# Weight tiles on multiples of 512 bytes, values fetched by head, stores spread: one change to a two-layer attention trunk

## The chip, the cores and the metric

One core of a Trainium2 chip runs the whole program in one launch. The metric is the device time of that launch in microseconds (us). The kernel before has a median of 1944.94 us over 3 runs (1943.95 to 1949.24).

Engines: PE is TensorE (matrix products; PEld its weight loads), DVE is VectorE, ACT is ScalarE, POOL is GpSimd, SP issues most transfers. A matrix product has a stationary operand (128x128, loaded into the array) and a moving one (128 partitions x up to 512 columns).

## The reference

Two layers on 512 tokens of width 2048, all in float32. Layer 0 is differential attention with ALiBi (8 heads, two score maps each, values of 256), layer 1 forgetting attention (16 heads of 128) on keys, values and forget gates projected once from the output of layer 0. Each layer shifts and scales its input by vectors computed from `c`, gates its output with SiLU, and ends in a residual layer norm.

```python
c_act = silu(c)
for l in range(2):
    shift, scale, gate = split(c_act @ w_mod[l] + b_mod[l], 3)
    h = x * (1 + scale) + shift
    if l == 0:
        q, k, v, g = split(h @ a_w_in, 4)
        a = softmax(q1 @ k1.T + alibi) - lam * softmax(q2 @ k2.T + alibi)
        y = (rms_norm(a @ v) * (1 - lam_init) * silu(g)) @ a_w_out
    else:
        hk = x * (1 + scale_kv) + shift_kv
        k, v, zf = split(hk @ kv_w)                  # once
        F = cumsum(log_sigmoid(zf + b_f))
        q, g = split(h @ b_w_in, 2)
        p = softmax(q @ k.T + F[t] - F[s], causal)
        y = (p @ v * silu(g)) @ b_w_out
    x = layer_norm(sqrt(2) * x + gate * y)
```

(`DN_ALPHA` is 4 to the power of 1/4, the square root of 2.)

## The kernel before, in words

**Products.** Every large product is made of three in the fast 32-bit format: a float32 operand is split into a rounded part `hi` and the rest `lo`, and hi·hi, hi·lo and lo·hi are summed in PSUM (`products`, L340, lines L342 to L344; in the opening stage `product`, L889, line L894). Tokens lie transposed in 16 pairs `hh`, `hl` of 128 x 512.

**Weights.** `WeightStream` (L173) loads tiles of weights into four buffers `wst` on SP's queue, casts them to `whi` on ACT (L242) and subtracts to `wlo` on DVE (L243); both have three buffers. All these tiles have 1056 columns of 4 bytes, 4224 bytes in a partition, because the narrow pair (below) needs 4 x 264 columns; all others use 1024 of them, as two k-tiles of 512. In the program of before the pool of weights begins on a multiple of 512; `whi` lies 0, 128 and 256 bytes past a multiple of 512 in its three buffers, `wlo` 384, 0 and 128 bytes. The pools of tokens (`hh`, `hl`) and of 2048-byte tiles (`kpool`, tag K, where the last products' `held` weights lie too) are on multiples of 512, and so are all slices of 128 columns of them. The pool of the layer-0 attention starts 256 bytes past a multiple, that of the middle part (`npool`) puts its token sums `su` 128 bytes past one.

**Groups.** `group` (L488) runs one tile of weights after the other (eight steps of two k-tiles) over four PSUM banks. In a column group (Q, K; `natural=False`) a 128-column slice of the weight tile is stationary and the 512 tokens move; in a row group (V, gates, output projections) a slice of 128 tokens is stationary and the 512 weight columns move. A step is 4 banks x 2 k-tiles x 3 = 24 products; after each bank's 6 products, a burst, `tick` (L472) takes the next entry of a list `pieces`: score, softmax, turning and value pieces of the attention of the heads before, which so run between the bursts. `background` streams the modulation vectors on DVE the same way: products with `cact` are summed over partitions by turning 512 columns in blocks of 32 and reducing them (`mod_rows`, L627: `V.transpose` L638, `V.tensor_reduce` L639).

**The middle.** After layer 0 the values' columns are computed partly as two factored pairs of blocks (`seven_products`, L1716: seven products of half blocks in place of eight, from sums of tokens made in `combine`, L1669). First the wide pair (512 columns each), then the narrow one (264 columns: 248 of values and 16 of forget-gate logits). Each ends by storing eight blocks into `v_dram` from ACT's queue (`store`, L1727, issue at L1729). The last 16 columns of the narrow one are copied to `fcols` (L1731); `forget_logits` (L1819) turns them on PE as an entry of `pieces` in the next group.

**Layer 1.** For each of eight pairs of heads a group projects Q and gates. In its last step the values of the pair (128 partitions x 4 blocks x 256 columns) come from `v_dram` into `vld` (`load_pair`, L1941) and are split to `vbh`, `vbl` (`split_pair`, L1950, by `split`, L336, whose lines are L337 on ACT and L338 on DVE); the pieces of the pair run in the next group (`attention_pair`, L2060).

**Order.** The opening stage is written out by hand for four engines (L41 to L44). After it the framework orders each engine's instructions and gives a tile's buffer out again when its last reader is done; each engine then works strictly in that order, so that an instruction that waits holds back those behind it, transfers on the same queue included.

Of the kernel before, what the change touches and what calls it, by code (L numbers as in the profile page):

```python
# [172 lines left out]
class WeightStream:  # L173
# [24 lines left out]
    def tile(self, name, dtype, bufs):  # L198
        return self.pool.tile([P, 1056], dtype, name=name, tag=name, bufs=bufs)
# [77 lines left out]
def tile_yoco(  # L277
# [77 lines left out]
    ones = const.tile([P, P], F32, name="ones")  # L355
    G.memset(ones, 1.0)
# [15 lines left out]
    pcol = const.tile([P, 38], F32, name="pcol")  # L372
# [22 lines left out]
    def load_parameters():  # L395
        prow = rows["p"] = kpool.tile([P, T], F32, name="prow", tag="K")[:38, 0:P]
        nc.sync.dma_start(prow[0:16, :], ln_g[0].rearrange("(a p) -> a p", p=P))
        nc.sync.dma_start(prow[16:32, :], ln_b[0].rearrange("(a p) -> a p", p=P))
        for k, lam in enumerate((a_lam_q1, a_lam_q2, a_lam_k1, a_lam_k2)):
            nc.sync.dma_start(prow[32 + k : 33 + k, :], lam)  # L400
        nc.sync.dma_start(prow[36:38, :], a_subln_g[0].rearrange("(a p) -> a p", p=P))

    def parameter_columns():
        pt = tr_bank()
        PE.transpose(pt[:, 0:38], rows["p"], ident[0:38, 0:38])
        V.tensor_copy(pcol, pt[:, 0:38])
# [220 lines left out]
    def mod_rows(pool, dst, bias, ones_at):  # L627
# [6 lines left out]
        def steps(n, acc):  # L634
            if n == 0:
                red.append(pool.tile([P, P], F32, name="mred", tag="mred", bufs=1)[:, 0 : 16 * last])
            t = pool.tile([P, 512], F32, name="mturn", tag="mturn", bufs=1)
            V.transpose(t, acc)  # L638
# [22 lines left out]
    with tc.tile_pool(name="start", bufs=2, reuse_waits="tile") as sp, tc.manual_schedule(engines=MANUAL):  # L661
# [164 lines left out]
        def op_o(i):  # L826
            if any(r not in d_list[: cnt["d"]] for r in d_list if r[0] == i):
                return False
            if any(r not in e_list[: cnt["e"]] for r in e_list if r[0] == i) or pm_of(i) is None:
                return False  # L830
            nk = sets[i][1]
            for v in range(2):
                for q in range(nk):
                    PE.matmul(
                        pms[i][:, nk * v + q : nk * v + q + 1], acc2[i][:, v, q * P : (q + 1) * P], ones[:, 0:1],
                        start=not rows_pe[i], stop=True, skip_group_check=True,
                    )
            return True
# [159 lines left out]
    for dst, src, col, bias, one in (  # L998
# [4 lines left out]
        steps = mod_rows(ap, dst, bias[col : col + n * D], one)  # L1003
# [7 lines left out]
    def vectors(pool, wanted):  # L1011
        segs = []
        for dst, src, col, bias, one in wanted:
            n = len(one)
            steps = mod_rows(pool, dst, bias[col : col + n * D], one)
# [39 lines left out]
    def attention_a(h, lead=3, late=(), spread=False):  # L1055
# [5 lines left out]
        def score(i, comp):  # L1061
            def fn():
# [450 lines left out]
    def open_n():  # L1513
# [3 lines left out]
        zp.extend((pool, None, pool.tile([P, TB, 4, 6], F32, name="nstats")))  # L1517
# [145 lines left out]
    fcols = npool.tile([P, TB, B_HEADS], F32, name="fcols")  # L1663
# [51 lines left out]

    def seven_products(one, two):  # L1716
# [10 lines left out]
        def store(t, b, col):  # L1727
            n = w if col == c0 else nv
            nc.scalar.dma_start(v_dram[b * P : (b + 1) * P, col : col + n], t[:, :n])  # L1729
            if n < w:  # L1730
                S.copy(fcols[:, b, :], t[:, n:w])  # L1731
                fz["cols", b] = fcols[:, b, :]
# [6 lines left out]
        for a in range(8 // per):  # L1739
            tiles = ws.get(one, a)  # L1740
            for k in range(per):
# [3 lines left out]
                add(p1, lambda b: plain(2 * s, b), tiles, k, s == 0, s == 7)  # L1745
        p2 = banks((partial(tr_bank, "p2"), partial(o_bank, "p2")))
# [16 lines left out]
        for s in range(8):  # L1763
# [21 lines left out]
            if last:  # L1785
# [25 lines left out]
    F = const.tile([P, TB, B_HEADS], F32, name="F")  # L1811
# [7 lines left out]
    def forget_logits():  # L1819
        pt = tr_bank()  # L1820
        for b in range(TB):
            PE.transpose(pt[0:B_HEADS, b * P : (b + 1) * P], fz["cols", b], ident)
# [73 lines left out]
    pieces.extend([None] * 3 + [forget_logits, None, forget_sums] + [None] * 14 + [columns_of_f])  # L1896
# [43 lines left out]

    def load_pair(p):  # L1941
        v = bp.tile([P, TB, 256], F32, name="vld", tag="vld", bufs=1)
        nc.sync.dma_start(v, v_dram[:, 256 * p : 256 * (p + 1)].rearrange("(j p) e -> p j e", p=P))
        cur[p, "vld"] = v
# [5 lines left out]
    def split_pair(p):  # L1950
        vh = bp.tile([P, TB, 256], F32R, name="vbh", tag="vbh", bufs=1)
        vl = bp.tile([P, TB, 256], F32R, name="vbl", tag="vbl", bufs=1)
        split(vh, vl, cur[p, "vld"])
        cur[p, "vB"] = (vh, vl)
        for hd in (2 * p, 2 * p + 1):
# [104 lines left out]
    def attention_pair(p):  # L2060
        sa, ra, da, ta, na, va = attention_b(2 * p)
        sb, rb, db, tb, nb, vb = attention_b(2 * p + 1)
        if p == 7:

            return [
                None, None, sa[0], sa[1], ra[0], [sa[2], ra[1]], da[0], [sa[3], da[1]], [ra[2], ta[0]], [sb[0], ta[1]],
# [4 lines left out]
            [], [], [sa[0]], [sa[1]], [ra[0]], [sa[2], ra[1]], [da[0]], [sa[3], da[1]], [ra[2]], [sb[0], ta[0]],  # L2071
# [207 lines left out]
```

## Time and profile before

| | |
|---|---|
| median of 3 runs | 1944.94 us |
| the profiled execution | 1943.87 us |
| its span | 1942.1 us |
| PE busy | 1925.2 us, 8827 products |
| DVE, ACT, POOL busy | 1432.8, 768.6, 2.3 us |
| HBM traffic | 206 GB/s over the span |

How to read it: a page of the profile has the busy time of each engine, the span in slices, and the chain of work that ended last. Views answer to a part of it. A row of the timeline has the start in us, the duration in us, the engine, the line, the operation, the tiles (out<-in), the shape and a count. A row of groups has line, engine, operation, tiles, shape and count, then the time busy and the mean ns of one, then the idle time ahead of it. A row of waits has who waited for whom, us in total, times, and the longest. A row of stages has the window, its length, and for PE, PEld, DVE, ACT and POOL the busy time with the count; then the granted PE clock, the share of time that the transfer engines are busy, and GB/s. A row of one tile has the operation and count, min/median/max ns, and first and last start. Products overlap: a product's own 0.39 us reaches into the next, so that the distance between starts is what counts.

### The profile page before, as it was taken

To read this page: it belongs to the slowest core of one execution; us is meant where nothing else is said; L and a number is where in the kernel's file an instruction comes from. 1 tells how busy PE (TensorE), PEld (TensorE's weight loads), DVE (VectorE), ACT (ScalarE), POOL (GpSimd) and SP (SyncE) were. 2 spreads that over 40 slices of the span, in tenths; PEclk is the share of its full clock that TensorE was granted. 3 is DMA by queue.
4 is the path that set the end of the run, shared out by engine and by line. 5 is a ranking of instruction groups with operands and counts; after the bars stand their busy time and mean duration, and the time that the engine had idled before them with its cause. 6 is when DMAs were issued, how large, how long until landed. Compare 5 with 4: busy or idle time off the path is not lost.

```text
span 1942.1 us, 25642 instructions
## 1 busy us (share of the span) xinstructions
PE 1925.2 (99%) x8827; PEld 1581.7 (81%) x8827; DVE 1432.8 (74%) x2665; ACT 768.6 (40%) x1304; POOL 2.3 (0%) x11
## 2 busy tenths in 40 slices
PE   8999999999999999999999999999999999999998
PEld 6888888888888888888888888888888888888887
DVE  7893578777776768657687876868866666687978
ACT  3656344333332334521265543224344434453122
POOL 0000000000000000000000000000000000000000
PEclk9999999999999999999999999999999999999999
DMA  9993566676767676476658678776654455555852
GB/s 347 385 322 94 157 189 188 207 236 187 232 192 227 196 222 182 125 259 221 195 175 288 193 213 282 268 260 192 215 162 149 145 153 156 152 153 182 310 166 107
DMA packets 346770, 402.23 MB, mean 207 GB/s; under 512 B 77016, under 2 KB 254324, under 8 KB 345360
## 3 DMA queue, kind: packets, MB, share of 16 engines
q1 hardware_dynamic: 342960, 395.20, 64.0%
q10 hardware_dynamic: 3680, 5.40, 0.9%
q8 instruction: 69, 1.13, 0.2%
q14 instruction: 61, 0.50, 0.1%
HBM read 363.46 MB, written 37.04 MB: 206 GB/s over the span
## 4 chain that ended last, share of the span: by engine, by line
PE 93%; DVE 3%; DMA 2%; SPq 1%; issue 0%; ACT 0%; ACTq 0%; DVEq 0%
PE acc L343 25%; PE acc L344 25%; PE acc L342 25%; PE acc L894 4%; PE sc L894 2%; PE sc L342 2%; PE sc L344 2%; PE sc L343 2%; PE o L342 1%; PE o L344 1%; PE o L343 1%; PE o L894 1%; SPq L742 1%; DVE wlo L243 1%; DMA v_dram<-vfirst 0%
## 5 line engine op out<-in xcount | busy, mean ns | idle before, releaser
L242 ACT CAST whi<-wst 128x1024 fp32r<-128x1024 f32 (+2 forms) x299 | 310.3, 1039 | 598.2 <-PE acc L344 240.7
L243 DVE TENSOR_TENSOR wlo<-wst,whi 128x1024 fp32r<-128x1024 f32 (+2 forms) x299 | 361.4, 1210 | 215.3 <-ACT whi L242 212.9
L344 PE MATMUL acc<-hh,wlo 128*128 128x512 f32 x1184 | 469.1, 396 | 0.0
L343 PE MATMUL acc<-hl,whi 128*128 128x512 f32 x1184 | 468.1, 395 | 0.0
L342 PE MATMUL acc<-hh,whi 128*128 128x512 f32 x1184 | 465.0, 393 | 0.0
L342 PE MATMUL acc<-whi,hh 128*128 128x512 f32 (+1 forms) x912 | 358.1, 393 | 0.2 <-DVE htmp L1762 0.2
L343 PE MATMUL acc<-wlo,hh 128*128 128x512 f32 (+1 forms) x912 | 355.2, 389 | 0.0
L344 PE MATMUL acc<-whi,hl 128*128 128x512 f32 (+1 forms) x912 | 353.7, 388 | 0.0
L342 PEld LDWEIGHTS acc<-hh,whi 128*128 128x128 f32 x1184 | 224.8, 190 | 48.3 <-issue 0.5
L344 PEld LDWEIGHTS acc<-hh,wlo 128*128 128x128 f32 x1184 | 222.3, 188 | 49.6
L343 PEld LDWEIGHTS acc<-hl,whi 128*128 128x128 f32 x1184 | 222.6, 188 | 47.0
L344 PEld LDWEIGHTS acc<-whi,hl 128*128 128x128 f32 x912 | 171.1, 188 | 39.3 <-DVE hl L1585 0.2
L342 PEld LDWEIGHTS acc<-whi,hh 128*128 128x128 f32 x912 | 171.3, 188 | 37.5 <-DVE htmp L1762 0.6
L343 PEld LDWEIGHTS acc<-wlo,hh 128*128 128x128 f32 x912 | 171.5, 188 | 34.4
L612 DVE SCALAR_TENSOR_TENSOR macc<-ms,cact,macc 128x512 f32<-128x512 f32 x180 | 134.0, 745 | 20.1 <-DMA ms<-in_kv_w_mod_dram 11.8
L792 DVE SCALAR_TENSOR_TENSOR sacc<-sms,cact,sacc 128x512 f32<-128x512 f32 (+1 forms) x128 | 90.0, 703 | 5.0 <-DMA sms<-in_w_mod_dram 1.4
L559 DVE SCALAR_TENSOR_TENSOR macc<-ms,cact,macc 128x1024 f32<-128x1024 f32 x60 | 76.8, 1281 | 13.0 <-DMA ms<-in_w_mod_dram 12.5
L1088 ACT ACTIVATE e<-e,mn 128x128 f32<-128x128 f32 (+3 forms) x64 | 36.0, 563 | 113.5 <-DVE mn L1084 106.8
L1987 ACT ACTIVATE eb<-eb,mnb 128x128 f32<-128x128 f32 (+1 forms) x64 | 36.0, 562 | 69.2 <-DVE mnb L1984 68.8
L894 PE MATMUL acc<-wlo,hh 128*128 128x512 f32 x128 | 50.2, 401 | 0.1
L894 PE MATMUL acc<-whi,hl 128*128 128x512 f32 x128 | 49.5, 394 | 0.0
L894 PE MATMUL acc<-whi,hh 128*128 128x512 f32 x128 | 49.2, 393 | 0.0
(402 smaller groups left out, 2492.9 us busy)
## 6 DMA issues: line engine op xcount, KB each, us to landing
wst<-in_a_w_in_dram SPq DMA_DIRECT2D x240, 256.0 KB
ms<-in_w_mod_dram SPq DMA_DIRECT2D x96, 512.0 KB
ms<-in_kv_w_mod_dram SPq DMA_DIRECT2D x64, 512.0 KB
wst<-in_b_w_in_dram SPq DMA_DIRECT2D x128, 256.0 KB
wst<-in_kv_w_dram SPq DMA_DIRECT2D x59, 512.0 KB
sms<-in_w_mod_dram SPq DMA_DIRECT2D x56, 512.0 KB
wst<-in_a_w_out_dram SPq DMA_DIRECT2D x32, 512.0 KB
wst<-in_b_w_out_dram SPq DMA_DIRECT2D x32, 512.0 KB
```

Of the source, the lines that this page charges most:

```text
L242: self.nc.scalar.copy(hi, st)
L243: self.nc.vector.tensor_tensor(lo, st, hi.bitcast(F32), op=ALU.subtract)
L342: PE.matmul(dst, lhs[0], rhs[0], start=start, stop=False, skip_group_check=True)
L343: PE.matmul(dst, lhs[0], rhs[1], start=False, stop=False, skip_group_check=True)
L344: PE.matmul(dst, lhs[1], rhs[0], start=False, stop=stop, skip_group_check=True)
L559: ins = V.scalar_tensor_tensor(acc, w, one, acc, op0=ALU.mult, op1=ALU.add)
L612: ins = V.scalar_tensor_tensor(acc, w, cact[:, kt : kt + 1], acc, op0=ALU.mult, op1=ALU.add)
L742: (queue or nc.sync).dma_start(mtile[n][:, kq : kq + step, v, :], rows.rearrange("(k p) n -> p k n", p=P))
L792: V.scalar_tensor_tensor(acc, w, sc, acc, op0=ALU.mult, op1=ALU.add)
L894: PE.matmul(bank[n, bk], l, r, start=start, stop=stop, skip_group_check=True)
L1088: S.activation(e[:, :w], e[:, :w], AF.Exp, bias=mn, scale=-1.0, accum_out=rs)
L1987: S.activation(e[:, :w], e[:, :w], AF.Exp, bias=mn, scale=-1.0, accum_out=rs)
```

## The change

1. The tiles of split weights (`whi`, `wlo`, and `held` is as before) get 1152 columns in place of 1056: 4608 bytes. `wst` keeps 1056.
2. To make room and to bring other tiles onto multiples of 512: the constant tile `ones` goes; a column of ones becomes column 38 of `pcol` and the square of ones a part of the tile `prow`. `nstats` takes 512 bytes in place of 384. `mn` and `rsum` have eight buffers in place of two. `fcols` goes: the logits are copied into `F` and turned from there.
3. `mod_rows` takes its turning tile from its caller: in layer 0 it turns 256 columns at a time in its own buffer, in the middle 512 in the two `htmp` buffers.
4. The values of layer 1 are fetched by head: the even head's with `load_pair` and `split_pair`, the odd head's loaded at the third entry of the pair's pieces and split at the ninth. `vld` has 2048 bytes in place of 4096.
5. The last four of the wide pair's eight stores are kept in `unsent`, and issued one at a time among the first products of the narrow pair, from its third k-tile on. `forget_logits` comes three entries later.

```diff
     def tile(self, name, dtype, bufs):
-        return self.pool.tile([P, 1056], dtype, name=name, tag=name, bufs=bufs)
+        return self.pool.tile([P, 1056 if dtype == F32 else 1152], dtype, name=name, tag=name, bufs=bufs)
...
-    ones = const.tile([P, P], F32, name="ones")
-    G.memset(ones, 1.0)
...
+    pcol = const.tile([P, 40], F32, name="pcol")
+    one = pcol[:, 38:39]
+    G.memset(one, 1.0)
...
+        prow = kpool.tile([P, T], F32, name="prow", tag="K")
+        rows["ones"] = prow[:, P : 2 * P]
+        G.memset(rows["ones"], 1.0)
+        prow = rows["p"] = prow[:38, 0:P]
...
-        PE.matmul(pt[:, 0:2], ones, lam2, start=True, stop=True)
+        PE.matmul(pt[:, 0:2], rows["ones"], lam2, start=True, stop=True)
...
-            t = pool.tile([P, 512], F32, name="mturn", tag="mturn", bufs=1)
-            V.transpose(t, acc)
-            V.tensor_reduce(
-                red[0][:, 16 * n : 16 * n + 16], t.rearrange("p (j q) -> p j q", q=32), axis=mybir.AxisListType.X, op=ALU.add
-            )
+            tag, bufs, w = turned
+            for c in range(0, 512, w):
+                t = pool.tile([P, w], F32, name="mturn", tag=tag, bufs=bufs)
+                V.transpose(t, acc[:, c : c + w])
+                V.tensor_reduce(
+                    red[0][:, 16 * n + c // 32 : 16 * n + (c + w) // 32], t.rearrange("p (j q) -> p j q", q=32),
+                    axis=mybir.AxisListType.X, op=ALU.add,
+                )
...
+        steps = mod_rows(ap, dst, bias[col : col + n * D], one, ("mturn", 1, 256))
...
+            steps = mod_rows(pool, dst, bias[col : col + n * D], one, ("htmp", 2, 512))
...
-                    st["mn", i] = ap.tile([P, 2], F32, name="mn", tag="mn", bufs=2)
-                    st["rs", i] = ap.tile([P, 2], F32, name="rsum", tag="rsum", bufs=2)
+                    st["mn", i] = ap.tile([P, 2], F32, name="mn", tag="mn", bufs=8)
+                    st["rs", i] = ap.tile([P, 2], F32, name="rsum", tag="rsum", bufs=8)
...
-        zp.extend((pool, None, pool.tile([P, TB, 4, 6], F32, name="nstats")))
+        zp.extend((pool, None, pool.tile([P, P], F32, name="nstats")[:, 0 : 24 * TB].rearrange("p (b f k) -> p b f k", b=TB, k=6)))
...
-                S.copy(fcols[:, b, :], t[:, n:w])
-                fz["cols", b] = fcols[:, b, :]
+                S.copy(F[:, b, :], t[:, n:w])
...
                 add(p1, lambda b: plain(2 * s, b), tiles, k, s == 0, s == 7)
+                if s >= 2 and unsent:
+                    unsent.pop(0)()
...
                     V.tensor_tensor(us[b], p7[b], us[b], op=ALU.add)
-                    store(us[b], 2 + b, c0)
                 for b in both:
                     V.tensor_tensor(diff[b], diff[b], second[b], op=ALU.add)
-                    store(diff[b], 2 + b, c1)
+                for b in both:
+                    for t, c in ((us[b], c0), (diff[b], c1)):
+                        if per == 2:
+                            unsent.append(partial(store, t, 2 + b, c))
+                        else:
+                            store(t, 2 + b, c)
...
-    pieces.extend([None] * 3 + [forget_logits, None, forget_sums] + [None] * 14 + [columns_of_f])
+    pieces.extend([None] * 6 + [forget_logits, None, forget_sums] + [None] * 14 + [columns_of_f])
...
+    def load_v(hd):
+        v = cur[hd, "vld"] = bp.tile([P, TB, 128], F32, name="vld", tag="vld", bufs=1)
+        nc.sync.dma_start(v, v_dram[:, 128 * hd : 128 * (hd + 1)].rearrange("(j p) e -> p j e", p=P))
+
+    def split_v(hd):
+        es = slice(128 * (hd % 2), 128 * (hd % 2) + 128)
+        vh, vl = cur[hd // 2, "vB"]
+        split(vh[:, :, es], vl[:, :, es], cur[hd, "vld"])
...
+        later_v, split_later = partial(load_v, 2 * p + 1), partial(split_v, 2 * p + 1)
...
-            [], [], [sa[0]], [sa[1]], [ra[0]], [sa[2], ra[1]], [da[0]], [sa[3], da[1]], [ra[2]], [sb[0], ta[0]],
+            [], [], [sa[0], later_v], [sa[1]], [ra[0]], [sa[2], ra[1]], [da[0]], [sa[3], da[1]], [ra[2], split_later], [sb[0], ta[0]],
```

More of the change, by code (lines that the diff above doesn't have):

```diff
@@ L1661, in back_k @@
             nc.sync.dma_start(KTs[b], k_dram[b])
-    fcols = npool.tile([P, TB, B_HEADS], F32, name="fcols")
+    F = const.tile([P, TB, B_HEADS], F32, name="F")
     upper, lower = {}, {}
@@ L1939, in evac_b @@
         return fn
+    def load_v(hd):
[5 more added lines that the diff above has]
+        split(vh[:, :, es], vl[:, :, es], cur[hd, "vld"])
     def load_pair(p):
-        v = bp.tile([P, TB, 256], F32, name="vld", tag="vld", bufs=1)
-        nc.sync.dma_start(v, v_dram[:, 256 * p : 256 * (p + 1)].rearrange("(j p) e -> p j e", p=P))
-        cur[p, "vld"] = v
+        load_v(2 * p)
         for hd in (2 * p, 2 * p + 1):
@@ L1952, in split_pair @@
         vl = bp.tile([P, TB, 256], F32R, name="vbl", tag="vbl", bufs=1)
-        split(vh, vl, cur[p, "vld"])
         cur[p, "vB"] = (vh, vl)
+        split_v(2 * p)
         for hd in (2 * p, 2 * p + 1):
```

16 lines of the change are left out of this document (6 added, 10 removed).

## The prediction, on record before the result

> **What bounds the kernel now.** I read the page's busy times and its chain first, then the waits of PE, then the stages, then groups by shape, and last the start times of single products.
>
> ```profile
> span 1942.1 us, 25642 instructions
> PE 1925.2 (99%) x8827; PEld 1581.7 (81%) x8827; DVE 1432.8 (74%) x2665; ACT 768.6 (40%) x1304; POOL 2.3 (0%) x11
> PEclk9999999999999999999999999999999999999999
> PE 93%; DVE 3%; DMA 2%; SPq 1%; issue 0%; ACT 0%; ACTq 0%; DVEq 0%
> ```
>
> TensorE is busy for 99% of the span at full granted clock, and the chain that ended last is 93% PE. So the time is the number of matrix products times the distance from one start to the next, plus a little idle time. The waits of PE and two stages say where that little is:
>
> ```profile
> PE tr L1822 <- ACT fcols L1731: 1.9, 2, 1.1
> PE p L343 <- DVE wlo L243: 0.9, 1, 0.9
> PE p L342 <- ACT whi L242: 0.3, 1, 0.3
> ...
> 1150.00:1210.00 60.00, 56.71 (x402) 52.64 (x402) 41.78 (x66) 22.52 (x30) 0.00 (x0) 1.00 0.85 273
> ...
> 1500.00:1850.00 350.00, 350.00 (x1582) 286.31 (x1581) 253.87 (x535) 135.48 (x255) 0.10 (x1) 1.00 0.57 178
> ```
>
> Between 1150 and 1210 us (the two factored pairs) PE idles 60.00 - 56.71 = 3.3 us, and the three waits above are 3.1 of it. In the forgetting-attention stage PE idles not at all. No wait in the middle can return more than these 3.3 us; a large change must come from the distance between products.
>
> That distance is not the same everywhere. In a column group (Q and K: the stationary operand is a 128-column slice of the weight tile, the token tile moves) one step of two k-tiles is 24 products. Five step starts:
>
> ```profile
> 1050.70 0.40 PE L342 MATMUL acc<-hh,whi 128*128 128x512 f32 x1
> 1056.31 0.39 PE L342 MATMUL acc<-hh,whi 128*128 128x512 f32 x1
> 1061.86 0.39 PE L342 MATMUL acc<-hh,whi 128*128 128x512 f32 x1
> 1067.41 0.40 PE L342 MATMUL acc<-hh,whi 128*128 128x512 f32 x1
> 1073.02 0.39 PE L342 MATMUL acc<-hh,whi 128*128 128x512 f32 x1
> ```
>
> The steps take 5.61, 5.55, 5.55 and 5.61 us: a period of three, which is the number of `whi`/`wlo` buffers. By the program's own addresses these steps use `whi` at 128, 0, 256 and 128 bytes past a multiple of 512, and `wlo` at 0, 384, 128 and 0. The tokens always lie on multiples. In a row group (V and gates: the weight tile moves, a token slice is stationary) the same view gives:
>
> ```profile
> 672.39 0.40 PE L342 MATMUL acc<-whi,hh 128*128 128x512 f32 x1
> 678.00 0.39 PE L342 MATMUL acc<-whi,hh 128*128 128x512 f32 x1
> 683.51 0.40 PE L342 MATMUL acc<-whi,hh 128*128 128x512 f32 x1
> 689.10 0.40 PE L342 MATMUL acc<-whi,hh 128*128 128x512 f32 x1
> 694.70 0.39 PE L342 MATMUL acc<-whi,hh 128*128 128x512 f32 x1
> ```
>
> 5.61, 5.51, 5.59 and 5.60 us, with `whi` at 256, 128, 0, 256 and `wlo` at 128, 0, 384, 128. The fast step is the one whose `wlo` is on a multiple. The mean over the three buffers is 5.57 us in both kinds of group. Now the only products of before that have both operands on multiples of 512, the held tiles of the last projection:
>
> ```profile
> 1902.58 0.39 PE L342 MATMUL acc<-held,hh 128*128 128x512 f32 x1
> 1904.89 0.39 PE L343 MATMUL acc<-held,hh 128*128 128x512 f32 x1
> ...
> 1912.21 0.39 PE L342 MATMUL acc<-held,hh 128*128 128x512 f32 x1
> ...
> 1914.93 0.39 PE L342 MATMUL acc<-whi,hh 128*128 128x512 f32 x1
> ```
>
> Right after a misplaced weight tile the first 10 take 2.31 us, 231 ns each; once settled, 12 take 2.72 us, 227 ns each, or 5.44 us for 24.
>
> **The change part by part. Tiles on multiples of 512.** 1152 columns of 4 bytes are 4608 = 9 x 512 bytes where 1056 were 8.25 x 512; `ones` takes its 512 bytes out ahead of the tokens, so these stay on multiples; 384 bytes of statistics become 512 and the 128 bytes of `mn`/`rsum` become 512, so the token sums `su`, and `ah`/`al`, come onto multiples too. How many products this touches:
>
> ```profile
> L344 PE MATMUL acc<-hh,wlo 128*128 128x512 f32 x1184 | 469.1, 396 | 0.0
> L343 PE MATMUL acc<-hl,whi 128*128 128x512 f32 x1184 | 468.1, 395 | 0.0
> L342 PE MATMUL acc<-hh,whi 128*128 128x512 f32 x1184 | 465.0, 393 | 0.0
> L342 PE MATMUL acc<-whi,hh 128*128 128x512 f32 x880 | 348.8, 397 | 0.0
> L343 PE MATMUL acc<-wlo,hh 128*128 128x512 f32 x880 | 346.1, 393 | 0.0
> L344 PE MATMUL acc<-whi,hl 128*128 128x512 f32 x880 | 344.6, 392 | 0.0
> L894 PE MATMUL acc<-wlo,hh 128*128 128x512 f32 x128 | 50.2, 401 | 0.1
> ...
> L344 PE MATMUL tr<-whi,hl 128*128 128x512 f32 x16 | 6.3, 392 | 0.0
> ```
>
> The six large groups hold 3552 + 2640, and the 27 smaller ones from x128 to x16 (opening stage 672, wide pair 240, one block of the last projection 192) another 1104: 7296 products, 304 steps of 24. If every one settled as the held ones do, a step would lose 5.57 - 5.44 = 0.13 us: 39.5 us. Two deductions. First, a run that has been interrupted does not start settled: by the held rows ten products at 231 instead of 227 ns, 0.04 us. Attention pieces cut the runs: 8 heads with 8 score and 4 value pieces and 16 heads with 4 and 2 make 192, so 192 x 0.043 = 8.3 us. Second, the opening stage is already better:
>
> ```profile
> 67.27 5.49 PE acc L894 x24
> ```
>
> Its 672 products (28 steps) lose 0.05 rather than 0.13 each: 2.2 us less. Left: **29.0 us**. The narrow pair's products (264 columns, 1056 bytes) stay off the multiples and get nothing.
>
> **Stores and forget logits.** `forget_logits` goes from the fourth to the seventh product burst, three bursts of 6 products or 4.2 us later, against a wait of 1.9 us at L1822: **1.9 us** goes, unless the copies into `F` come later as well. Half of the wide pair's eight stores move behind the first products of the narrow pair. They sit on ACT's queue, and behind them there stand the copies at L1750 and the casts `whi`. At best the remaining 1.2 us of the three waits go; at worst one store holds ACT once for as long as the longest one on the chain:
>
> ```profile
> 1198.34 8.70 DMA v_dram<-vfirst
> ```
>
> I take 0, since the same four stores only move by a few us within a stretch whose transfers run at 0.85.
>
> **Values by head.** The cost of one 128x1024 split against two 128x512 ones:
>
> ```profile
> L1943 SPq DMA_DIRECT2D vld<-v_dram x8: 366/367/425, 1335.8 to 1699.3; - x8
> L337 ACT CAST vbh<-vld x8: 1047/1052/1054, 1340.5 to 1749.0; 128x1024 fp32r<-128x1024 f32 x8
> L338 DVE TENSOR_TENSOR vbl<-vld,vbh x8: 1216/1226/1227, 1341.6 to 1750.1; 128x1024 fp32r<-128x1024 f32 x8
> ...
> L337 ACT CAST kb<-kT x16: 611/615/623, 1339.0 to 1720.3; 128x512 fp32r<-128x512 f32 x16
> L338 DVE TENSOR_TENSOR kb<-kT,kb x16: 648/672/690, 1340.3 to 1725.1; 128x512 fp32r<-128x512 f32 x16
> ```
>
> ACT pays 2 x 615 - 1052 = 178 ns and DVE 2 x 672 - 1226 = 118 ns more per pair, 1.4 and 0.9 us over eight pairs, and SP issues eight more loads of 367 ns, ahead of later weight loads. All of it lies beside PE: in 1500 to 1850 us DVE works 254 and ACT 135 of 350 us and PE misses nothing. There is one new wait: the second head's split stands on ACT and DVE six bursts (36 products, 8.3 us) after its load was issued; casts of weights queue behind it. A landing within 8.3 us costs nothing; without cover the eight pairs would cost 8 x 0.3 = 2.4 us.
>
> **The rest at nothing.** Turning 256 columns at a time adds two small operations to each of 12 segments:
>
> ```profile
> L638 DVE STREAM_TRANSPOSE mturn<-macc x20: 669/710/714, 278.0 to 1292.1; 128x512 f32<-128x512 f32 x20
> L338 DVE TENSOR_TENSOR vl<-acc,vh x20: 415/419/425, 408.7 to 797.2; 128x256 fp32r<-128x256 f32 x20
> ```
>
> A 256-wide DVE operation takes 419 where a 512-wide one takes 672, so 166 ns are fixed: 12 x 2 x 0.17 = 4 us of DVE, hidden by its idle quarter; uncovered, 4 us. `mturn` in the `htmp` buffers can make DVE wait for one life of a temporary, about one us, eight times, beside PE. Eight instead of two `mn`/`rsum` buffers remove waits that PE never shows. The memset moves on an idle POOL; the ones column and `F` are the same operations at another address.
>
> **Sum** against the profiled execution: 1943.87 (span 1942.1 plus 1.8 around it) - 29.0 - 1.9 = 1913.0. The median of the runs, 1944.94, lies 1.07 above it, so **1914.0 us**.
>
> **The rivals.** (1) *Only the moving side gains.* The load of the stationary operand runs beside the current product and may be hidden, so that only the 3456 products with moving weights (144 steps; 384 of them, 16 steps, opening) gain: 144 x 0.13 - 16 x 0.08 - 4.2 = 13.2, with the stores 15.1: 1929.8 us. For it: PEld is busy for 81%, not 100%. Against it: in the column groups only the stationary slice is off, and 5.61 against 5.55 follows its place. The Trainium skill says this in "TensorE: Matmul & The Clock Gate", Part 2, on LDWEIGHTS: two separate read ports, so that loading the next weights takes nothing from the running product. The column rows disagree with it by 0.06 us a step.
>
> (2) *No effect of place.* The period of three could belong to the rotation of the buffers (waits, refills) and not to their addresses: then only 1.9 us go, 1943.0 us. Against it: the step of each place repeats to 0.01 us in the rows above. The Trainium skill's "SBUF — State Buffer", Specifications, has lines of 16 bytes as the grain of access, of which all these places are multiples; by that none would differ, and the rows by slot speak against it.
>
> (3) *A collision: slower.* In the row groups the step with `whi` on a multiple (5.59) is slower than the one with `whi` at 128 (5.51). If what costs there is that moving and stationary operand start on the same place within 512 bytes, the change makes this the rule everywhere. At the slowest step shown, 5.61, all 304 steps lose 0.04 us, 12.2 us: 1943.87 + 12.2 - 1.9 + 1.07 = 1955.2. It decides if steps with both tiles on multiples exceed 5.57. Against it: the held rows, both operands on multiples, have 5.44.
>
> **How the numbers follow.** Forecast 0.75, rival (1) 0.15, (2) 0.06, (3) 0.04. The low end is every step settled and all three waits gone, 1943.87 - 39.5 - 3.3 + 1.07, about 1902, so 1903; the high end takes in rival (1) and one bad store in a part, 1935. About 0.3% (5.8 us) is what a measurement of this kernel can tell from no change: faster 0.90, same 0.06, slower 0.04.
>
> **What would show it.** In the changed kernel: steps of 24 in both kinds of group near 5.44 to 5.48 us with no period of three; the wait at L1822 gone; PE without gaps in the attention stage although `vld` is loaded 16 times; DVE's and ACT's counts up, their waits on PE longer. It would be wrong if the column groups keep 5.55 or more (then the stationary side does not pay), if row groups sit at 5.59, or if ACT shows waits on `vld` followed by PE waiting on `whi`.

## The result, and the profile after

The changed kernel takes 1917.34 us (median of 4 runs, 1914.19 to 1921.48), against 1946.04 us of the kernel before in the same runs (1943.95 to 1949.24): a ratio of 0.9852, 95% interval 0.9828 to 0.9877. It is faster by 1.5%. Its profiled execution took 1916.57 us. Line numbers grow along the changed kernel (L894 is now L900).

The page of the changed kernel, its span, its busy times and its chain:

```profile
span 1914.8 us, 25687 instructions
...
PE 1895.5 (99%) x8827; PEld 1579.7 (83%) x8827; DVE 1435.3 (75%) x2697; ACT 769.9 (40%) x1312; POOL 2.3 (0%) x12
...
PE 89%; DVE 4%; DMA 4%; SPq 1%; issue 1%; ACT 0%; DVEq 0%; ACTq 0%
```

The span is 27.3 us shorter, and PE is busy 29.7 us less with the same 8827 products. But the chain's share of PE fell from 93 to 89%, and DVE and DMA rose from 5 to 8%: something else now ends last somewhere. First the products. The starts of successive steps in a row group and in a column group of the changed kernel (start in us, us of one; the 23 products between are left out):

```profile
669.28 0.39 PE L342 MATMUL acc<-whi,hh 128*128 128x512 f32 x1
...
674.72 0.39 PE L342 MATMUL acc<-whi,hh 128*128 128x512 f32 x1
...
680.16 0.39 PE L342 MATMUL acc<-whi,hh 128*128 128x512 f32 x1
...
1030.86 0.39 PE L342 MATMUL acc<-hh,whi 128*128 128x512 f32 x1
...
1036.30 0.39 PE L342 MATMUL acc<-hh,whi 128*128 128x512 f32 x1
...
1041.73 0.39 PE L342 MATMUL acc<-hh,whi 128*128 128x512 f32 x1
```

5.44 us in both kinds of group, with no period of three. In the opening stage a run of 24 on the chain has come down from 5.49 to the same length:

```profile
67.48 5.44 PE acc L900 x24
```

Over all 512-column products, where the next one starts within 300 ns, the mean distance from start to start fell from 231.71 to 227.56 ns. With 7584 of these products that is 7584 x 4.15 ns = 31.5 us. The span returned 27.3 us of them, so about 4 us went elsewhere in this execution. A second profile of the changed kernel (`after_again` below) has a span of 1912.0 us, 30.1 us shorter than before, so that part of the 4 us is scatter between executions. The waits of PE in the changed kernel (us in total, times, longest) say where to look for the rest:

```profile
PE acc L344 <- DVE wlo L243: 3.2, 4, 1.2
...
PE tr L654 <- DVE mred L644: 1.2, 1, 1.2
```

The wait of `tr` on `fcols` (1.9 us) and that on `whi` (0.3 us) are gone; 3.2 us on `wlo` and 1.2 us on `mred` are new. By stretches (length, then busy us of PE, PEld, DVE, ACT, POOL with counts, granted clock, DMA share, GB/s), first one row of the kernel before, then three of the changed kernel:

```profile
1210.00:1380.00 170.00, 170.00 (x736) 137.84 (x735) 131.50 (x153) 53.54 (x67) 0.00 (x0) 1.00 0.75 251
...
1150.00:1210.00 60.00, 58.90 (x376) 53.26 (x375) 39.76 (x58) 19.83 (x26) 0.00 (x0) 1.00 0.83 280
1210.00:1380.00 170.00, 165.53 (x730) 135.00 (x728) 134.10 (x179) 55.91 (x76) 0.00 (x0) 1.00 0.72 237
1500.00:1850.00 350.00, 350.00 (x1607) 291.72 (x1606) 258.72 (x523) 133.62 (x246) 0.10 (x1) 1.00 0.59 185
```

Between 1210 and 1380 us PE now idles 4.5 us, where it idled not at all; in the attention stage it still idles not at all. The chain of the changed kernel in the middle shows what DVE was doing ahead of those waits (start, us, what):

```profile
1187.01 6.14 DMA v_dram<-us
1193.28 0.76 DVE macc L560
1194.07 1.30 DVE macc L562
1195.38 6.25 DMA ms<-in_w_mod_dram
...
1231.82 4.64 DMA ms<-in_w_mod_dram
1236.61 1.14 issue
1237.75 1.22 DVE wlo L243
```

Here the chain runs along transfers of `ms`, the tiles of the modulation stream, of 4.6 to 6.4 us each, and from each to a DVE product that consumes it (`macc`). DVE works in order, so a `wlo` that stands behind a `macc` waits for a transfer. Products are faster there and the transfers are not: the stretch moves 237 GB/s, against 251 before.

### The profile page after: what moved, and what is told of

It is laid out like the page before. It is cut to its first block, busy times and chain, and to the rows that moved or that the text cites. A ratio compares the mean times of both kernels' runs of the same rounds, so it can differ in the third digit from the quotient of the medians.

```text
span 1914.8 us, 25687 instructions
## 1 busy us (share of the span) xinstructions
PE 1895.5 (99%) x8827; PEld 1579.7 (83%) x8827; DVE 1435.3 (75%) x2697; ACT 769.9 (40%) x1312; POOL 2.3 (0%) x12
## 4 chain that ended last, share of the span: by engine, by line
PE 89%; DVE 4%; DMA 4%; SPq 1%; issue 1%; ACT 0%; DVEq 0%; ACTq 0%
PE acc L342 24%; PE acc L343 24%; PE acc L344 23%; PE acc L900 4%; DMA ms<-in_w_mod_dram 2%; PE sc L900 2%; PE sc L344 2%; PE sc L343 2%; PE sc L342 2%; PE o L344 1%; PE o L342 1%; PE o L343 1%; PE o L900 1%; DVE wlo L243 1%; SPq L748 1%
## 5 line engine op out<-in xcount | busy, mean ns | idle before, releaser
L344 PE MATMUL acc<-hh,wlo 128*128 128x512 f32 x1184 | 461.0, 390 | 3.2 <-DVE wlo L243 3.2
L343 PE MATMUL acc<-hl,whi 128*128 128x512 f32 x1184 | 461.5, 390 | 0.0
L342 PE MATMUL acc<-whi,hh 128*128 128x512 f32 (+1 forms) x912 | 353.9, 389 | 0.2
L900 PE MATMUL acc<-wlo,hh 128*128 128x512 f32 x128 | 50.0, 399 | 0.5 <-DVE wlo L262 0.5
L900 PE MATMUL acc<-whi,hl 128*128 128x512 f32 x128 | 49.3, 393 | 0.0
L900 PE MATMUL acc<-whi,hh 128*128 128x512 f32 x128 | 49.1, 393 | 0.0
```

What stands on the lines that cost most here:

```text
L342: PE.matmul(dst, lhs[0], rhs[0], start=start, stop=False, skip_group_check=True)
L343: PE.matmul(dst, lhs[0], rhs[1], start=False, stop=False, skip_group_check=True)
L344: PE.matmul(dst, lhs[1], rhs[0], start=False, stop=stop, skip_group_check=True)
L900: PE.matmul(bank[n, bk], l, r, start=start, stop=stop, skip_group_check=True)
```

## The experiments

Two theories were at stake for the gain. Theory A: a 512-column product costs 227 ns when both operands lie on multiples of 512 (or of some smaller power of two), more otherwise, and this pays whether the operand moves or is stationary. Its rivals were those of the prediction: only the moving side pays, place does not matter, or a common place is itself the cost. For the 4 us given back: A, the faster products have outrun the transfers; the rival, the later forget logits and stores of the same change push work into the way.

**Whole change without the weight tiles.** `e1_weights_back`: `whi` and `wlo` get their 1056 columns back, and a gap keeps every other pool on its new place.

```diff
-        return self.pool.tile([P, 1056 if dtype == F32 else 1152], dtype, name=name, tag=name, bufs=bufs)
+        return self.pool.tile([P, 1056], dtype, name=name, tag=name, bufs=bufs)
...
+    wpool.tile([P, 64], F32, name="gap", tag="gap", bufs=1)
     ws = WeightStream(nc, wpool)
```

> All of the change but its first part: whi and wlo at 1056 columns again, with a gap of 256 bytes so that every other tile keeps the place it has after the change; whi then lies 256, 384 and 0, wlo 128, 256 and 384 bytes past a multiple of 512. Theory (the place of the split weights makes the gain): steps of 24 products take 5.51 to 5.61 us again with a period of three, products of 512 columns are 231.5 ns apart in the mean, the time is 1942 to 1946 us, and PE has none of the changed kernel's waits for wlo between 1195 and 1280 us, because slower products leave DVE the time. Rival (stores, logits, values by head or the other tiles' places give a good part): 1925 to 1938 us, with steps that stay below 5.55.

Measured: 1944.19 us against 1945.64 of before, ratio 0.9993 [0.9984, 1.0002]. The period of three is back; four column steps:

```profile
1050.01 0.40 PE L342 MATMUL acc<-hh,whi 128*128 128x512 f32 x1
...
1055.62 0.39 PE L342 MATMUL acc<-hh,whi 128*128 128x512 f32 x1
...
1061.16 0.39 PE L342 MATMUL acc<-hh,whi 128*128 128x512 f32 x1
...
1066.72 0.40 PE L342 MATMUL acc<-hh,whi 128*128 128x512 f32 x1
```

5.61, 5.54 and 5.56 us, a mean distance of 231.71 ns, to the hundredth that of before. The weight tiles' place is the whole gain, and all other edits together are worth nothing that can be measured while the products are slow. The waits on `wlo`, which were expected to go, shrank from 3.2 to 1.1 us, and 2.4 us on `mred` are there.

**Multiples of 256 only.** `e2_1088_columns`: 1088 columns, 8.5 x 512 bytes, so that the buffers lie alternately at 0 and 256.

```diff
-        return self.pool.tile([P, 1056 if dtype == F32 else 1152], dtype, name=name, tag=name, bufs=bufs)
+        return self.pool.tile([P, 1056 if dtype == F32 else 1088], dtype, name=name, tag=name, bufs=bufs)
```

> 1088 in place of 1152 columns: the six weight buffers lie alternately 0 and 256 bytes past a multiple of 512, everything else as in the changed kernel. Theory (a multiple of 256 is enough, as the column steps with whi at 256 and the settled rows with wlo on a multiple hinted): steps of 5.44 us in every buffer, the same time as the changed kernel, 1914 to 1921 us. Rival (it must be 512): the steps whose whi or wlo is at 256 take 5.5 us or more, half of the gain goes, 1928 to 1935 us.

Measured: 1915.41 us, ratio 0.9847 [0.9824, 0.987]. The median step is 5.440 us at 0 and at 256, in both kinds of group. What counts has a grain of at most 256 bytes.

**Tokens off their place.** `e3_tokens_off`: on top of the 1088 columns, 128 bytes ahead of the token pool and 384 behind it, so that `hh` and `hl` lie 128 past a multiple of 512 and the weight tiles at 0 or 256.

```diff
+    gap1 = ctx.enter_context(tc.tile_pool(name="gap1", bufs=1))
+    gap1.tile([P, 32], F32, name="gap1")
     hpool = ctx.enter_context(tc.tile_pool(name="hpool", bufs=32))
+    gap2 = ctx.enter_context(tc.tile_pool(name="gap2", bufs=1))
+    gap2.tile([P, 96], F32, name="gap2")
```

> On top of the 1088 columns, 128 bytes of nothing ahead of the token pool and 384 behind it: only the token tiles hh and hl (and what is held in their pool) lie 128 bytes past a multiple, split weights stay at 0 or 256. Theory (either operand off a multiple of 256 costs its product): every step slows down, row groups and column groups alike, to 5.6 us or more, 304 steps by 0.16 us: 1960 to 1975 us, slower than before the change. Rival A (only the weights' place counts): as without the shift, 1914 to 1921 us. Rival B (a collision between the places of both operands, off is good): not slower than 1921 us.

Measured: 1950.07 us, ratio 1.0022 [1.0012, 1.0031], slower than before but by less than expected. Column steps:

```profile
1044.83 0.40 PE L346 MATMUL acc<-hh,whi 128*128 128x512 f32 x1
...
1050.43 0.40 PE L346 MATMUL acc<-hh,whi 128*128 128x512 f32 x1
...
1056.03 0.40 PE L346 MATMUL acc<-hh,whi 128*128 128x512 f32 x1
```

5.60 us in this group, and mostly 5.57 to 5.60 in other column groups; row steps, where the tokens are the stationary operand, have a median of 5.58. With well-placed weight tiles the gain is lost altogether.

**One tile of two off.** `e9_only_wlo_off` moves `wlo` alone by 128 bytes.

```diff
+        if name == "wlo" and self.gap:
+            self.pool.tile([P, 32], F32, name="gap", tag="gap", bufs=1)
+        t = self.pool.tile([P, 1056 if dtype == F32 else 1088], dtype, name=name, tag=name, bufs=bufs)
+        if name == "wlo" and self.gap:
+            self.pool.tile([P, 96], F32, name="gap2", tag="gap2", bufs=1)
+            self.gap = False
+        return t
```

> This kernel is the changed one with split weight tiles of 1088 columns and the three wlo buffers 128 bytes further on: whi at 0 or 256, wlo at 384 or 128 bytes past a multiple of 512, all else on its place. Only the 8 of 24 products of a step that read wlo have an operand off a multiple of 256. Theory A (each product pays for its own two operands and nothing for its neighbours): 8 products by about 7 ns, so steps of 5.49 to 5.50 us in both kinds of group; 304 steps by 0.055 us are 17 us, about 1933 us. Theory B (a misplaced operand also slows the products beside it, as the steps of before with whi on a multiple and wlo off it, 5.55 in column and 5.59 us in row groups): 304 steps by 0.11 to 0.15 us, about 1950 to 1960 us less what the other places of before cost, so near 1947. A stationary operand whose place is free would leave the column groups at 5.44 us.

Measured: 1939.09 us against 1945.27, ratio 0.9963 [0.995, 0.9975]; a median step of 5.547 us in both kinds of group. That is neither theory's number: the first is too low by 0.05 us a step and by 6 us, and the second is right for the steps of column groups only, and too high by 8 us. The single products of a column step show why (start, us):

```profile
1043.65 0.39 PE L349 MATMUL acc<-hh,whi 128*128 128x512 f32 x1
1043.88 0.40 PE L350 MATMUL acc<-hl,whi 128*128 128x512 f32 x1
1044.11 0.40 PE L351 MATMUL acc<-hh,wlo 128*128 128x512 f32 x1
1044.35 0.39 PE L349 MATMUL acc<-hh,whi 128*128 128x512 f32 x1
1044.57 0.40 PE L350 MATMUL acc<-hl,whi 128*128 128x512 f32 x1
1044.80 0.40 PE L351 MATMUL acc<-hh,wlo 128*128 128x512 f32 x1
```

Taken to the nanosecond over the settled column steps, `hh,whi` lasts 227 from its start to the next one's, `hl,whi` 232 to 233 and `hh,wlo` 234. Two products of three are slow for one misplaced tile: the one that uses it and the one before it, beside which it is loaded. So a price per misplaced operand is the wrong picture. Which of the two neighbours pays for what, the starts alone don't say.

In the row groups of this run the picture is not so clean, and the same places do not even have one price. Two steps of 24, from an early group and from the last projection:

```profile
385.11 0.40 PE L349 MATMUL acc<-whi,hh 128*128 128x512 f32 x1
...
390.71 0.40 PE L349 MATMUL acc<-whi,hh 128*128 128x512 f32 x1
...
1784.60 0.39 PE L349 MATMUL acc<-whi,hh 128*128 128x512 f32 x1
...
1790.10 0.39 PE L349 MATMUL acc<-whi,hh 128*128 128x512 f32 x1
```

The first step takes 5.60 us and the second 5.49 to 5.50, where most row steps take 5.547; each value repeats until something interrupts the products. So unlike places make a product slow, but how slow depends on something else that these runs do not show.

**All four off by the same.** If the loading of one tile disturbs the moving of another only where their places differ, then it would not matter where they lie, as long as they lie alike. `e11_all_128_off` has the tokens at 128 as in `e3_tokens_off` and moves `whi` and `wlo` by 128 bytes too.

```diff
+        if name == "whi" and self.gap:
+            self.pool.tile([P, 32], F32, name="gap3", tag="gap3", bufs=1)
         t = self.pool.tile([P, 1056 if dtype == F32 else 1088], dtype, name=name, tag=name, bufs=bufs)
```

> Split weight tiles of 1088 columns, and all four operand tiles 128 bytes past a multiple of 256: hh and hl at 128, whi and wlo at 128 or 384 past a multiple of 512. Moving and stationary operand then lie on the same place within 256 bytes, but on no multiple of it. The held tiles and the other operands keep their places. Theory A (what counts is a multiple of 256): every product has both operands off, so steps of 5.58 us or more in both kinds of group and 1950 to 1960 us. Theory B (what counts is that the two operands lie on the same place within 256 bytes, as the slow products beside a change of place in the run before suggest): steps of 5.44 us in both kinds of group and about 1917 to 1919 us, with only the products that mix held tiles and tokens slower.

Measured: 1920.23 us against 1945.93, ratio 0.9866 [0.9849, 0.9883]. No operand of a step lies on a multiple of 256, and the steps are these:

```profile
665.61 0.39 PE L353 MATMUL acc<-whi,hh 128*128 128x512 f32 x1
...
671.05 0.39 PE L353 MATMUL acc<-whi,hh 128*128 128x512 f32 x1
...
1043.89 0.39 PE L353 MATMUL acc<-hh,whi 128*128 128x512 f32 x1
...
1049.33 0.39 PE L353 MATMUL acc<-hh,whi 128*128 128x512 f32 x1
```

5.44 us again, in both kinds of group, and a time a little above the 1917 to 1919 us of theory B. Theory A falls in the form that it had: not the multiple pays, but that moving and stationary operand lie on the same place within 256 bytes. In this kernel most held tiles of the last projection stayed at 0 while the tokens went to 128, and the products `held,hh` went the other way: a mean of 231.7 ns, 227.4 in the changed kernel's second profile (`after_again` below). The token sums of the wide pair (`su`, `sl`), which stay on multiples, went the same way: products of weight tiles with them lie 231.7 to 234.9 ns apart in the mean here, 226.1 to 227.0 in the changed kernel, and 227.0 to 230.7 in `e3_tokens_off`, where only the tokens are off. Only differences of 128 bytes and of none were tried; what 32 or 64 would do is open.

**Where the 4 us went.** Three kernels take the two edits of the middle back, together and one by one: `e4_stores_at_once` both, `e6_only_stores_at_once` the spread stores, `e7_only_logits_early` the later logits.

```diff
-                        if per == 2:
-                            unsent.append(partial(store, t, 2 + b, c))
-                        else:
-                            store(t, 2 + b, c)
+                        store(t, 2 + b, c)
...
-    pieces.extend([None] * 6 + [forget_logits, None, forget_sums] + [None] * 14 + [columns_of_f])
+    pieces.extend([None] * 3 + [forget_logits, None, forget_sums] + [None] * 14 + [columns_of_f])
```

> The changed kernel with the wide pair's stores all issued at once and forget_logits three bursts earlier, as before. Theory (the waits of PE for wlo between 1195 and 1280 us, 3.2 and 1.2 us, come from faster products running into a stretch whose transfers and DVE can go no faster): those waits stay within 2 us of their size and the wait of the logits on their columns comes back with 1 to 2 us: 1916 to 1921 us, no different from the changed kernel by more than 3 us. Rival (moved stores and logits cause them): the waits for wlo go and the time is 1911 to 1914 us.

> The changed kernel with the wide pair's stores issued at once; the logits stay at their later place. If the spread stores cause the waits for wlo that the changed kernel has and the run with both undone has not: PE waits less than 1.2 us for wlo, and the logits' wait stays away: 1912 to 1915 us. If the later logits cause them: 3 us of waits for wlo remain, 1915 to 1919 us.

> The other half: stores spread as in the changed kernel, logits three bursts earlier as before. If the later logits cause the waits for wlo: those fall below 1.2 us and a wait of 1 to 2 us for the columns F returns, 1913 to 1916 us. If the spread stores do: 3 us of waits for wlo and 1 to 2 us for F, 1916 to 1920 us.

Measured: 1913.97 us (ratio 0.9832 [0.9815, 0.9848]), 1916.3 (0.9853 [0.9839, 0.9868]) and 1916.47 (0.9857 [0.9841, 0.9874]). The intervals overlap; the waits differ. Those of the kernel with early logits and spread stores:

```profile
PE tr L1834 <- ACT F L1739: 1.7, 2, 1.0
PE tr L654 <- DVE mred L644: 1.2, 1, 1.2
```

With early logits the wait on `F` is there (1.7, with both edits back 1.6 us), and that of `acc` on `wlo` is 0.3 us, 0.9 with both edits back; with late logits the wait on `F` is gone and that on `wlo` is 3.2 us, 2.7 where only the stores are at once. Where the products are slow, the same late logits leave waits on `wlo` of 1.1 (`e1_weights_back`), 1.0 (`e3_tokens_off`) and 0.2 us (`e9_only_wlo_off`). So in these profiles it takes both the faster products and the later logits to make the larger `wlo` waits, neither theory alone, and the spread stores do nothing that shows. This rests on one profile of each kernel, and the times do not tell the variants apart (1916.47 us with early logits alone lies above the 1913 to 1916 us that were expected with this reading). The logits' move seems to have traded one wait for another, within about a us.

The wait on `mred` is another matter. It is 1.2 us with early logits too, and 2.4, 2.1 and 1.2 us in the three kernels with slow products, while the kernel before has none. So it needs neither the faster products nor the later logits; which of the edits brings it is not shown.

**Making room for DVE.** Two kernels let the modulation stream run slower or start later, so that `wlo` need not stand behind it. `e5_slower_stream` gives it fewer of the bursts in the two groups and lets it end in the third:

```diff
-(k % 2 or k % 8 == 0) if g < 3 or k < 5 else 0
+(k % 2 or k % 16 == 0) if g < 3 or k < 9 else 0
...
-    pieces.extend([None] * 5 + [lambda: (end_of_sums(), fetch_rows(1))] + [None] * 5 +
+    pieces.extend([None] * 9 + [lambda: (end_of_sums(), fetch_rows(1))] + [None] * 5 +
```

> The changed kernel with the modulation stream (tiles ms of 512 KB, summed on DVE) slowed from 20 to 18 products in each of the next two groups, three of them moved into the group after those. Theory A (the stream asks for more than the transfers give once the products are faster, DVE waits for ms with wlo behind it): PE's waits of 3.2 us for wlo and 1.2 us for mred fall below 1.5 us together, 1912 to 1916 us. Theory B (the moved logits or stores cause the waits): they stay at 3 us or more, 1915 to 1920 us.

Measured: 1918.31 us, ratio 0.986 [0.9845, 0.9875]. The waits of its profile, which is that of its fastest execution (1913.53 us):

```profile
PE acc L342 <- DVE ql L1943: 2.2, 1, 2.2
...
PE acc L344 <- DVE wlo L243: 0.9, 2, 0.7
```

`e8_best_guess` combined 1088 columns, stores at once, early logits and a stream that starts later in the first group and also ends in the third:

```diff
-(k % 2 or k % 8 == 0) if g < 3 or k < 5 else 0
+(k % 2 or k % 8 == 0) if (k > 5, 1, k < 9)[g - 1] else 0
```

> A version that might beat the changed kernel: 1088 columns, stores at once, logits early, and the stream's products in the next group begin six bursts later, so that DVE does not stand at the first of them until a store has freed its sums; six of them go into the third group. Theory: of the 3 to 5 us of PE waits between 1150 and 1290 us some 2 go, 1910 to 1914 us; rival: the stream ends later and its last product holds PE in the third group, 1914 to 1920 us.

Measured: 1919.71 us, ratio 0.9867 [0.9852, 0.9881]. A miss like the one before:

```profile
PE acc L342 <- DVE ql L1940: 3.1, 1, 3.1
```

In both, the `wlo` waits shrink or go and one longer wait comes some 100 us later, at the start of a group of layer 1. PE waits there for a free accumulator: DVE empties it with `ql` (out of `acc`), and DVE stood behind products of the next stream, that of the gate vectors (`gs`), which waited for their transfers (0.9 and 1.3 us in `e8_best_guess`). That moving the first stream made the second one late is likely, but no run shows it.

**The cheapest variants beside the change.** `e10_1088_early_stores` is the kernel of 1088 columns with stores at once and early logits; `after_again` is the changed kernel, on the same chip.

> Split weight tiles of 1088 columns, the stores of the wide pair at once and the forget logits three bursts earlier: the two cheapest variants so far put together. If multiples of 256 do as well as multiples of 512, this is the variant with 1152 columns, stores at once and early logits (1914.0 us) again: 1912 to 1917 us. The waits of PE on wlo should be 1 us or less and the wait on F about 1.6 us. If it is slower than the changed kernel run beside it, the place in multiples of 512 has some worth of its own after all.

> The changed kernel itself, beside the two variants on the same chip: 1914 to 1920 us. If the variant with stores at once and early logits is better by what its waits say, about 3 us, it shows here as a difference of 0.15% between the two medians; otherwise the new waits of the changed kernel are worth no more than the noise.

Measured: 1915.27 us (1914.58 to 1916.51) and 1915.28 (1913.82 to 1916.32), ratios 0.9847 [0.9833, 0.9862] and 0.9846 [0.9831, 0.9861]. Equal. 1152 columns buy nothing over 1088 that shows (`e2_1088_columns` had 1915.41 us), and neither do the two edits of the middle. In these profiles the `wlo` wait of `acc` was 1.3 us with early logits and 1.8 in the changed kernel, in place of 3.2 before: one profile fixes such a wait to no better than a us or two. No kernel of the study beats the changed one by more than its runs scatter.

## Why the prediction was right, and where not

**The size.** 1914.0 us were forecast, 1917.34 measured, 1915.28 in the second set. The step of 24 came out at 5.44 us as the held rows said. On the 7296 products that the forecast counted, the mean distance was 230.86 ns in the opening stage (672 products) and 231.85 in the others (6624), and it became 227.87 and 227.49: 2.0 + 28.9 = 30.9 us, against 29.0 forecast. At the settled 5.440 us / 24 = 226.67 ns all of them together would have given 37.1 us, where the forecast has 39.5; what did not settle kept 6.2, where the forecast took off 8.3 + 2.2. This deduction is the term that was mis-sized, by 4.3 us, and the starting figure made up for 2.4 of it, so that the sum came out so near is in part luck. The forecast had counted each attention piece as a new, unsettled run of ten products; in the changed kernel six products after such a piece (at 305 us) lie 229 to 235 ns apart, and then they are settled.

**The cause.** The rule under the forecast, multiples of 512, was wrong in kind. The rows that it rested on, the held tiles, had both operands on multiples and so also on the same place; the trace of before had no long run of products with both operands off alike, so these rows could not tell the two apart. Rival (3), that a common place costs, was the exact opposite of the truth, and the held rows had refuted it rightly. The row steps from which it drew are not settled by any run: by the rule found, the step of 5.51 us (`whi` at 128, `wlo` at 0) has two of three products with unlike places and the one of 5.59 (`whi` at 0, `wlo` at 384) only one, and `e9_only_wlo_off` has 5.55 in most row groups at those latter places, and 5.49 and 5.60 in others. Settled steps with like places take 5.44 in every run; what unlike ones cost, from 0.05 to 0.17 us a step, depends on more than their number. So the prediction's word that the step of each place repeats holds within its rows, not from group to group.

**Rival (1), only the moving side,** is refuted by the column steps of `e9_only_wlo_off`, where only a stationary tile is off and the step is 5.547 us. It had been named with "TensorE: Matmul & The Clock Gate" of the Trainium skill, Part 2, two separate read ports so that loading weights takes nothing from the running product. These runs disagree with that as a rule for the time: 5 to 7 ns of 227 are lost where the two places differ. They do not show that the ports are the reason. **Rival (2), no effect of place,** is refuted by `e1_weights_back` against the changed kernel, 231.71 against 227.56 ns with the same other edits.

**The logits: 1.9 us forecast, about none kept.** The wait on the columns went as said. The step that failed is the sentence that the 1.9 us go "unless the copies into `F` come later as well": it looked for the price on ACT, and the waits that came in its place, on `wlo`, are on DVE. Why the later logits go with them is open. DVE's share of the same work, `forget_sums`, also comes later, but in the changed kernel it ends at 1216.5 us, and only one of the four waits on `wlo` (1.0 us, at 1211.9) falls within it. The other three (2.2 us) come from 1251 us on, and in between DVE waits for the stream's transfers:

```profile
DVE macc L562 <- DMA ms<-in_w_mod_dram: 5.9, 8, 1.8
```

By the distances of 300 ns and over between products, and what they exceed 227 ns by, the stretch from 1150 to 1400 us lost 4.4 us before and 7.8 after, but 5.9 in the second profile of the changed kernel and 7.2 in `e4_stores_at_once`, so this measure does not tell the variants apart either.

**The stores** were taken at 0 and are at 0: with them spread or at once the kernel takes 1916.5 or 1914.0 us where the logits are early and 1917.3 or 1916.3 where they are late, within the scatter.

**Values by head.** The cover held. The tile's rows in the changed kernel, min/median/max in ns:

```profile
L1955 SPq DMA_DIRECT2D vld<-v_dram x16: 366/384/472, 1319.7 to 1724.2; - x16
L337 ACT CAST vbh<-vld x16: 603/620/625, 1323.8 to 1732.9; 128x512 fp32r<-128x512 f32 x16
L338 DVE TENSOR_TENSOR vbl<-vld,vbh x16: 648/684/692, 1325.3 to 1733.6; 128x512 fp32r<-128x512 f32 x16
```

Twice 620 and twice 684 ns are within 10 and 24 ns of what was put down, and PE is busy for 350.00 of the stage's 350 us. **The rest at nothing** is confirmed as a whole by `e1_weights_back`, not edit by edit. The narrow pair's products (264 columns) stayed at 122.6 ns.

## What to carry to other kernels

When like products show a period equal to a number of buffers, look up the addresses: here 4 ns of 232 in every large product hung on the moving and the stationary tile lying on the same place within 256 bytes. Products of 264 columns were not tried. Lay out every tile that meets another on TensorE with a size that is a multiple of 256 bytes, and begin their pools alike. When products get faster, look again at the stretch that is bound by transfers, and when a step is moved, follow its followers on every engine, not only on the one that waited.

## What was not expected of the hardware

The price of unlike places is paid by a neighbour too: in the column groups of `e9_only_wlo_off` 232 to 233 ns for the product before the misplaced tile, 234 for its own. And it is not one price: row steps of that run take 5.49, 5.547 or 5.60 us at the same places. With like places the settled distances are 226 or 227 ns, and steps repeat to 1 ns.

In `e8_best_guess` a gap had an echo. The products around it, then two stretches of it (the column after the busy times is the granted clock):

```profile
1361.98 0.39 PE L344 MATMUL acc<-hh,wlo 128*128 128x512 f32 x1
1365.50 0.79 PE L342 MATMUL acc<-hh,whi 128*128 128x512 f32 x1 [3.14 <-DVE ql L1940]
1366.10 0.63 PE L343 MATMUL acc<-hl,whi 128*128 128x512 f32 x1
1366.52 0.63 PE L344 MATMUL acc<-hh,wlo 128*128 128x512 f32 x1
```

```profile
1355.00:1361.00 6.00, 6.00 (x28) 4.99 (x27) 4.42 (x4) 2.95 (x4) 0.00 (x0) 1.00 0.96 308
1366.00:1369.00 3.00, 3.00 (x8) 2.31 (x7) 3.00 (x5) 0.00 (x0) 0.00 (x0) 0.50 0.99 335
```

Two starts lie 3.5 us apart; after that the granted clock is 0.50 and the products start 427 ns apart until about 1371.2 us. Some 13 products at 0.2 us more each, about 2.6 us, come on top of the gap. In `e5_slower_stream` two starts 2.6 us apart were followed by one distance of 330 ns only, in `e6_only_stores_at_once` the same gap by some eight of 427, and in `e1_weights_back` 2.8 us were followed by slow products too. "TensorE: Matmul & The Clock Gate" of the Trainium skill, Part 1, has the clock halve after an idle window of some 3.4 us that runs freely; the 0.50 agrees, though here gaps of 2.6 us did it once, and once did not, so the length of the gap alone does not decide.
